# Start addresses of the up-projection's operand tiles in a hybrid decoder layer

## The chip, the core and the metric

The kernel runs on one core of a Trainium2 chip. The core has TensorE (matmul), VectorE, ScalarE and GpSimd, an on-chip memory SBUF of 128 partitions from which the engines read, a smaller memory PSUM into which TensorE writes, and DMA queues that move data between SBUF and the chip's main memory. The metric is the device time of one execution in microseconds (us); lower is better.

## What is computed

One decoder layer over 1024 positions of width 1024, in float32. Two groups of attention heads read the same normalised input; their outputs are joined, projected and added to the input; then comes an MLP with a squared ReLU:

```python
xn = rmsnorm(x, attn_norm_g)
proj = jnp.einsum('bsd,de->bse', xn, w_in)
...
x = x + jnp.einsum('bse,ed->bsd', mixed, w_out)
hn = rmsnorm(x, mlp_norm_g)
hid = jnp.square(jax.nn.relu(jnp.einsum('bsd,df->bsf', hn, w_up)))
x = x + jnp.einsum('bsf,fd->bsd', hid, w_down)
```

w_up is 1024 x 4096 and w_down 4096 x 1024.

## The kernel before

Every large product is made of matmuls in a rounded float32 type. To keep float32 accuracy each operand is split into a high and a low part (`split`, line 75: a copy into the rounded type gives the high part, a subtraction the low one), and a product is the sum of three matmuls: high by high, high by low, low by high. A matmul has a moving operand, which streams through the array, and a stationary one, the weights, which a separate load instruction puts into the array; here every matmul is preceded by its own load.

The stages are: an input projection; attention (lines 513 to 933), between whose pieces further projections and the first half of the output projection are woven; the rest of the output projection (from line 935); the **up phase** (`up`, line 1060, 16 calls); the **down phase** (`down`, line 1184, 16 calls).

Both MLP products use a Strassen-type scheme with seven products in place of eight. For the up phase the activations are prepared once: `bh[n]` and `bl[n]` (lines 967 to 969), n in the order UP = (1, 2, 3, 6, 7, 5, 4), are the high and low parts of seven combinations of quarters of the activations. These fourteen tiles, each of 4 x 512 floats per partition, are the moving operands. `up(j)` makes the seven combinations of weights of a block, splits each into a tile w with a high and a low half of 4 x 128 columns, and issues twelve matmuls per product (lines 1076 to 1079): for each of four k, w high by bh, w high by bl, w low by bh. That is 16 x 7 x 12 = 1344 matmuls of 512 columns.

All long-lived tiles come from `slot(tag, name, shape)`, line 146: tiles with the same tag share one place in SBUF, one after the other. Tags c0 to c13 lie in the pool "zr": bh and bl of the i-th product in UP are c(2i) and c(2i+1). Later the same tags hold the down phase's weight blocks (c0 to c9), two of its early operand sets and its running sums (c10 to c13). Tags w0 to w6 lie in the pool "zw", in the order of first use w2, w4, w3, two wor tiles, w0, w1, w5, w6. `w_slot` (line 1054) hands them out in rotation, seven tags for seven products, so that each product always gets the same tag: product 1 gets w5, 2 gets w6, 3 gets w0, 6 gets w1, 7 gets w2, 5 gets w3 and 4 gets w4. Before that, w0 and w1 hold the split weights of the output projection and w2 to w4 some of its other tiles; afterwards all seven hold blocks of the hidden values.

The order on each engine is the program's order, with priorities given by hand in the attention part; transfers are issued from SP's queue, for the down phase in a chain (`queue`, line 1157).

In the projection of line 458 the weights have 392 columns, the others 384; line 183 sets where the low half begins in its tile.

Of the kernel before, what the change touches and what calls it, by code (L numbers as in the profile page):

```python
# [16 lines left out]
P = 128  # L17
# [38 lines left out]
def hybrid_layer(  # L56
# [86 lines left out]
        tc.tile_pool(name="zl", bufs=1, side="left", reuse_waits="tile")  # L143
    )}

    def slot(tag, name, shape, dt=F32, pool=None):
        pool = o[pool or ("zw" if tag[0] == "w" else "zl")]
        return pool.tile([P] + shape, dt, tag=tag, name=name, bufs=1)


    X = [
        [slot(tag, "x", [2, 2, 512], F32R) for tag in tags]
        for tags in (("m1", "m2", "m3", "m4"), ("m0", "r0", "r1", "m5"))
    ]
# [705 lines left out]
    def mix_tiles(e):  # L860
        m = mixt[e] = slot(MIX[e], f"mix{e}", [2, S], F32R)
        mh[e], ml[e] = m[:, 0, :], m[:, 1, :]
# [7 lines left out]
    def out_weights(dt, e0):  # L870
        i = nout[0] = nout[0] + 1
        wr = o["zw"].tile([P, 4, P], F32, tag="wor", name="wor", bufs=2)
        nc.sync.dma_start(wr, w_o[dt][:, e0 : e0 + 4, :])
        w = slot(f"w{i % 2}", "wos", [2, 4, P], F32R)
        split(w[:, 0], w[:, 1], wr, nc.scalar, nc.gpsimd)
        return w[:, 0], w[:, 1]
# [154 lines left out]
    for dt in (1, 5, 2, 6, 3, 7):  # L1031
        w = out_weights(dt, 4)
# [273 lines left out]
    for i in range(len(STEPS)):  # L1306
        down(i)
        if STEPS[i][0] == len(PHASES) - 1 and late:
            name, dt, cs = late.pop(0)
# [65 lines left out]
```

## Time and profile before

| what | us |
|---|---|
| timed runs | 1091.99, 1091.10, 1089.88 |
| their median | 1091.1 |
| span of the profiled execution | 1090.4 |
| input projection and attention, to the last output product | 0 to 473 |
| up phase | 473.7 to 781 |
| down phase | 781 to 1086 |

The profiled execution is one more run; what is known of its time is the span, from its first to its last instruction. Rows of a view name the line, the engine and the tiles (written <- read, with buffer numbers left out). All matmuls of a helper have the helper's line, 73; what tells the phases apart is the tile they write: pu in the up phase, pd in the down phase, po in the output projection, ps and qps in the input projections. In a row of the timeline stand the start, the length and what ran; x8 says that eight instructions of one kind were merged. A matmul's own length covers its way through the array, and several are under way at once, so lengths of single matmuls overlap.

### The profile page before, as it was taken

The numbers are of one execution on the slowest core, as the hardware profiler recorded it, in microseconds if no ns is written. First come the engines' busy times: TensorE is split into PE (matmuls) and PEld (weight loads), VectorE is DVE, ScalarE is ACT, GpSimd is POOL, SyncE is SP. The second block draws the span as 40 slices with busy tenths as digits, with TensorE's granted clock in tenths as the row PEclk, the third lists the DMA queues.
The fourth block names the chain that finished last, engine by engine and source line by source line (L and its number), as shares of the span: only waits on it lengthen the run. The fifth ranks groups of instructions, "written<-read, shape, count | busy, mean of one in ns | idle before, by whom it ended". The sixth has DMA issues, their size and how long they took to land.

```text
span 1090.4 us, 15675 instructions
## 1 busy us (share of the span) xinstructions
PE 1080.1 (99%) x5556; PEld 933.8 (86%) x5556; DVE 782.7 (72%) x1321; ACT 571.4 (52%) x1022; POOL 362.4 (33%) x352
## 2 busy tenths in 40 slices
PE   9999999999999999999999999999999999999998
PEld 8999999999898888778888888888888888888886
DVE  8377677765776786898686869867665876674395
ACT  5558588776667766554545444353633433333331
POOL 4572523434445543333222232322212222231100
PEclk9999999999999999999999999999999999999999
DMA  9401212324657564663554543443998876665523
GB/s 292 156 22 53 69 36 65 113 70 150 230 164 252 182 209 173 212 231 126 193 184 174 188 160 135 149 170 145 335 390 308 305 288 224 237 231 177 176 87 116
DMA packets 96223, 195.69 MB, mean 179 GB/s; under 512 B 7392, under 2 KB 19856, under 8 KB 96144
## 3 DMA queue, kind: packets, MB, share of 16 engines
q1 hardware_dynamic: 95856, 194.54, 51.0%
q8 instruction: 44, 0.72, 0.3%
q14 instruction: 35, 0.29, 0.1%
q10 hardware_dynamic: 288, 0.15, 0.0%
HBM read 141.61 MB, written 53.04 MB: 179 GB/s over the span
## 4 chain that ended last, share of the span: by engine, by line
PE 86%; DMA 5%; DVE 4%; ACT 1%; issue 1%; POOL 1%; SPq 0%; DVEq 0%; ACTq 0%; POOLq 0%
PE pd L73 28%; PE pu L73 27%; PE ps L73 13%; PE po L73 4%; PE spb L73 3%; PE pvb L73 3%; PE tpb L739 3%; PE sp L73 1%; PE pv L73 1%; PE tpa L568 1%; DMA h_d<-h 1%; DMA xq<-in_x_dram 1%; DMA wr<-in_w_a_dram 1%; DMA rd_d<-rd 1%; PE ptk L334 1%
## 5 line engine op out<-in xcount | busy, mean ns | idle before, releaser
L73 PE MATMUL pd<-hx,wx 128*128 128x512 f32 (+1 forms) x1350 | 304.9, 388 | 0.0
L73 PEld LDWEIGHTS pd<-hx,wx 128*128 128x128 f32 x1350 | 252.7, 188 | 52.2
L73 PE MATMUL pu<-bh,wu 128*128 128x512 f32 x896 | 276.6, 390 | 0.3 <-POOL wu L80 0.2
L73 PEld LDWEIGHTS pu<-bh,wu 128*128 128x128 f32 x896 | 168.0, 188 | 36.1 <-POOL wu L80 0.6
L73 PE MATMUL ps<-w,x 128*128 128x384 f32 (+1 forms) x960 | 198.3, 344 | 0.5 <-ACT z L463 0.3
L73 PE MATMUL pu<-bl,wu 128*128 128x512 f32 x448 | 174.0, 389 | 0.0
L73 PEld LDWEIGHTS ps<-w,x 128*128 128x128 f32 x960 | 164.8, 189 | 3.8 <-ACT z L463 0.7
L77 ACT CAST hx<-hr 128x1024 fp32r<-128x1024 f32 x56 | 59.1, 1055 | 176.1 <-PE pd L73 170.9
L80 POOL TENSOR_TENSOR wx<-wda,wx 128x1024 fp32r<-128x1024 f32 x24 | 64.3, 2678 | 196.6 <-ACT wx L77 188.6
L80 DVE TENSOR_TENSOR hx<-hr,hx 128x1024 fp32r<-128x1024 f32 x56 | 72.5, 1302 | 72.5 <-ACT hx L77 72.5
L73 PEld LDWEIGHTS pu<-bl,wu 128*128 128x128 f32 x448 | 84.1, 188 | 17.7 <-issue 0.2
L73 PE MATMUL po<-mix,wos 128*128 128x512 f32 x384 | 94.2, 395 | 0.6 <-ACT pc L914 0.3
L73 PEld LDWEIGHTS po<-mix,wos 128*128 128x128 f32 x384 | 70.6, 188 | 15.7 <-ACT wos L77 1.1
L80 POOL TENSOR_TENSOR wu<-wus,wu 128x512 fp32r<-128x512 f32 x32 | 46.6, 1459 | 111.8 <-ACT wu L77 99.5
L80 POOL TENSOR_TENSOR wu<-wur,wu 128x512 fp32r<-128x512 f32 x32 | 44.1, 1378 | 102.7 <-ACT wu L77 100.1
L1047 DVE TENSOR_TENSOR ht<-hb 128x512 f32<-128x512 f32 x32 | 22.9, 757 | 62.8 <-ACT hb L1102 62.8
L80 POOL TENSOR_TENSOR w<-wr,w 128x384 fp32r<-128x384 f32 (+1 forms) x47 | 50.1, 1074 | 40.1 <-ACT w L77 28.6
L77 ACT CAST wu<-wus 128x512 fp32r<-128x512 f32 x64 | 37.9, 618 | 46.5 <-PE pu L73 39.2
L77 ACT CAST wx<-wda 128x1024 fp32r<-128x1024 f32 x56 | 58.5, 1049 | 6.8 <-DMA wda<-in_w_d_dram 6.5
L703 ACT ACTIVATE sb<-sb,nmb 128x128 f32<-128x128 f32 (+3 forms) x64 | 49.7, 778 | 22.1 <-DVE nmb L697 21.6
L406 DVE TENSOR_TENSOR ptl<-tpb,pth 128x512 fp32r<-128x512 f32 (+1 forms) x80 | 49.6, 631 | 15.1 <-ACT pth L405 14.3
L1101 ACT ACTIVATE hb<-hb 128x2048 f32<-128x2048 f32 x16 | 30.7, 1917 | 48.5 <-DVE hb L1050 48.4
(211 smaller groups left out, 1844.5 us busy)
## 6 DMA issues: line engine op xcount, KB each, us to landing
wda<-in_w_d_dram SPq DMA_DIRECT2D x34, 1024.0 KB, 8.7
hr<-hid_d SPq DMA_DIRECT2D x56, 512.0 KB, 5.7
wur<-in_w_u_dram SPq DMA_DIRECT2D x32, 512.0 KB, 4.4
hid_d<-ht SPq DMA_DIRECT2D x16, 1024.0 KB, 4.5
hid_d<-hb SPq DMA_DIRECT2D x16, 768.0 KB, 3.6
mix<-mixs_d SPq DMA_DIRECT2D x7, 1024.0 KB, 5.4
wr<-in_w_b_dram SPq DMA_DIRECT2D x32, 192.0 KB, 2.5
xq<-in_x_dram SPq DMA_DIRECT2D x8, 512.0 KB, 5.9
```

The source lines that it names most:

```text
L73: return nc.tensor.matmul(out, lhsT, rhs, start=start, stop=stop)
L77: hi_eng.copy(hi, src)
L80: lo_eng.tensor_tensor(out=lo, in0=src, in1=hi.bitcast(F32), op=ALU.subtract)
L334: nc.tensor.transpose(pt[:w, j * P : (j + 1) * P], x[:, 4 * c + j, col : col + w], ident)
L406: nc.vector.tensor_tensor(out=lo[:, cols], in0=pt[:, cols], in1=hi[:, cols].bitcast(F32), op=ALU.subtract)
L568: nc.tensor.transpose(tp[:, hh * P : (hh + 1) * P], pts[hh // 2][:, hh % 2, c0 : c0 + P], ident)
L703: nc.scalar.activation(pr[:, :nk], pr[:, :nk], AF.Exp, scale=-1.0, bias=nm[:, c : c + 1], accum_out=dn_b[p % 2][:, h, i : i + 1] if p < 3 ...
L739: nc.tensor.transpose(tp[:, c0 : c0 + P], probs[qi][:, kb * P : (kb + 1) * P], ident)
L1047: eng.tensor_tensor(out=out, in0=a, in1=b, op=ALU.subtract)
L1101: nc.scalar.activation(b, b, AF.Relu)
```

## The change

`slot` gets a table SHIFT. A tile whose tag is in it is allocated a little longer, and a view is handed out that begins SHIFT[tag] floats, 4 bytes each, behind the tile's start. The c tiles become 2112 floats long (8448 bytes in place of 8192), w2 becomes 1032 and w6 1056 floats long (in place of 1024). c9 and five of the w tags aren't in the table, and keep their length; what follows a longer tile in its pool moves along.

```diff
+    SHIFT = {
+        "w2": 8, "w6": 32,
+        "c0": 8, "c1": 40, "c2": 40, "c3": 8, "c4": 24, "c5": 56, "c6": 16,
+        "c7": 32, "c8": 48, "c10": 12, "c11": 20, "c12": 56, "c13": 24,
+    }
+
     def slot(tag, name, shape, dt=F32, pool=None):
         pool = o[pool or ("zw" if tag[0] == "w" else "zl")]
-        return pool.tile([P] + shape, dt, tag=tag, name=name, bufs=1)
+        if tag not in SHIFT:
+            return pool.tile([P] + shape, dt, tag=tag, name=name, bufs=1)
+        n, by = math.prod(shape), SHIFT[tag]
+        full = 1024 + by if tag[0] == "w" else 2048 + 64
+        t = pool.tile([P, full], dt, tag=tag, name=name, bufs=1)[:, by : by + n]
+        if len(shape) == 1:
+            return t
+        if len(shape) == 2:
+            return t.rearrange("p (a b) -> p a b", b=shape[1])
+        return t.rearrange("p (a b c) -> p a b c", b=shape[1], c=shape[2])
```

## The prediction

> **What bounds the kernel now.** I read the page's busy times first, then the chain of work that ended last in order of time, then the timeline of TensorE inside the up phase.
>
> ```profile
> PE 1080.1 (99%) x5556; PEld 933.8 (86%) x5556; DVE 782.7 (72%) x1321; ACT 571.4 (52%) x1022; POOL 362.4 (33%) x352
> PEclk9999999999999999999999999999999999999999
> L73 PE MATMUL pu<-bh,wu 128*128 128x512 f32 x896 | 276.6, 390 | 0.3 <-POOL wu L80 0.2
> L73 PE MATMUL pu<-bl,wu 128*128 128x512 f32 x448 | 174.0, 389 | 0.0
> ```
>
> TensorE is busy 99% of the span at full granted clock, and the 1344 up matmuls (896 with a high part bh moving, 448 with a low part bl) hardly wait for anybody. The 390 ns are one matmul's own duration; they overlap, so the price of one is the distance between two starts. The chain gives that:
>
> ```profile
> 487.15 178.00 PE pu L73 x784
> 665.15 1.72 PE pms L73 x4
> 666.86 114.29 PE pu L73 x504
> 781.15 300.57 PE pd L73 x1326
> 1081.75 0.71 DVE pd L1290
> ```
>
> From 487 to 1082 us the chain is nothing but matmuls: 178.00/784 = 227.0 ns each in the up phase, 300.57/1326 = 226.7 ns in the down phase. Whatever changes the distance between two starts in the up phase moves the end one for one; 1 ns on all 1344 is 1.34 us, or 0.12%. No other engine is near:
>
> ```profile
> 487.00:665.00 178.00, 177.85 (x785) 147.32 (x786) 135.96 (x193) 83.34 (x112) 53.67 (x40) 1.00 0.46 169
> ```
>
> This stretch has TensorE busy for 177.85 of 178 us, VectorE for 135.96, ScalarE for 83.34, GpSimd for 53.67.
>
> **What one matmul costs beside its columns.** Four runs of undisturbed matmuls, from the timeline of TensorE (start, length, matmuls in the row):
>
> ```profile
> 26.68 11.60 PE L73 MATMUL qps<-w,x 128*128 128x384 f32 x66
> 43.70 6.74 PE L73 MATMUL ps<-w,x 128*128 128x392 f32 x37
> 353.02 0.34 PE L73 MATMUL spb<-k2z,q1b 128*128 128x384 f32 x1
> 353.31 0.28 PE L73 MATMUL pvb<-ptl,vb 128*128 128x256 f32 x1
> ...
> 354.14 0.28 PE L73 MATMUL pvb<-pth,vb 128*128 128x256 f32 x1
> 500.20 0.62 PE L73 MATMUL pu<-bh,wu 128*128 128x512 f32 x2
> 500.65 0.39 PE L73 MATMUL pu<-bl,wu 128*128 128x512 f32 x1
> 500.88 0.62 PE L73 MATMUL pu<-bh,wu 128*128 128x512 f32 x2
> ```
>
> A row ends with the last matmul's own 0.34 us, so 384 columns cost (11.60-0.34)/65 = 173.2 ns and 392 columns (6.74-0.34)/36 = 177.8 ns. The 256-column row starts lie seven steps apart (six rows are left out): 0.83/7 = 118.6 ns. In the up phase the pattern high, low, high repeats after 0.68 us, so three cost 680 ns. From 512 against 384 a column costs (226.7-173.2)/128 = 0.418 ns; 512 columns are 213.9 ns, which leaves a **gap of about 12.8 ns per matmul** that isn't streaming. Each matmul loads new weights while its predecessor runs, so the gap may well come from two reads of SBUF at once. That gap is all that the change can touch: 1344 x 12.8 = 17.2 us.
>
> **The change, part by part.** (1) Addresses. No instruction, DMA or wait is written or dropped; slot() hands out a view that starts later in a longer tile, and SP's and POOL's queues keep their order. The allocator puts every w and c slot of the old kernel 224 bytes past a multiple of 256. The longer c slots are 8448 bytes, 33 x 256, so the tiles keep that base and the offsets alone count: bh1 0, bl1 128; bh2 128, bl2 0; bh3 64, bl3 192; bh6 32, bl6 96; bh7 160, bl7 224; bh5 16, bl5 48; bh4 192, bl4 64. w2 comes first in its pool, is 32 bytes longer and starts 32 later, so w0 to w5 all land on 0; w6 lands on 128. There are seven products and seven w slots in rotation, so product 2 always has w6 and the six others a slot at 0. Products 1 and 2 keep one moving tile at their weights' place and one 128 away; the five others (5 x 192 = 960 matmuls) get two new distances each.
>
> (2) What a distance is worth. The old up phase has one place for everything, so it can't show it. One place in the trace has another: line 183 puts the low weights w of the 392-column projection at column 400, 1600 bytes, thus 64 bytes off modulo 256, while 384-column ones lie at 1536, 6 x 256. There every third moving operand is at another place than its weights. By the terms above 392 columns should cost 392 x 0.418 + 12.8 = 176.7 ns; the row says 177.8, that is **1.1 ns more**, not less. (Since 392 columns also end differently, part of this may be length.) A gap that came from equal places should have shrunk there. The smallest gap in a row is that of the 256-column run, 118.6 - 107.0 = 11.6 ns, 1.2 less. The worst run of undisturbed up matmuls is this one, just after a wait:
>
> ```profile
> 477.20 0.40 PE L73 MATMUL pu<-bl,wu 128*128 128x512 f32 x1
> 477.44 0.63 PE L73 MATMUL pu<-bh,wu 128*128 128x512 f32 x2
> 477.91 0.39 PE L73 MATMUL pu<-bl,wu 128*128 128x512 f32 x1
> 478.13 0.63 PE L73 MATMUL pu<-bh,wu 128*128 128x512 f32 x2
> 478.60 0.39 PE L73 MATMUL pu<-bl,wu 128*128 128x512 f32 x1
> 478.83 0.40 PE L73 MATMUL pu<-bh,wu 128*128 128x512 f32 x1
> 479.06 0.39 PE L73 MATMUL pu<-bl,wu 128*128 128x512 f32 x1
> 479.29 0.62 PE L73 MATMUL pu<-bh,wu 128*128 128x512 f32 x2
> ```
>
> Nine steps in 2.09 us are 232.2 ns each, 5.5 above the steady 226.7, at unchanged places; afterwards the stream falls back into the 680 ns pattern. So the gap depends on how the two reads stand to each other in time, and a stream of equal matmuls settles on one rhythm. I expect the shifted streams to settle as well. Their price lies between 0 (same rhythm) and the 392 row's 1.1 ns on the 960 matmuls with new distances, 1.1 us; I take the middle, **+0.5 us**. Both ends of the whole range are -12.8 ns (gap gone) and +5.5 ns (never settled).
>
> The row first, then the rule: each matmul here carries its own weight load and 12.8 ns of gap. The Trainium skill, "TensorE: Matmul & The Clock Gate", Part 2, step 1, says that the array reads moving values and weights through two independent SBUF ports, so that loading weights takes nothing from a running matmul. By it the places are worth exactly 0 and the sum would be 1091.1. The gap in the trace is no proof against it, since it could be a fixed cost of exchanging weights.
>
> (3) The same slots outside the up phase. 15 of 16 wos weight tiles of the output projection are in w0 and w1 and move by 32 bytes against the mix tiles: 360 matmuls, at +1.1 ns 0.4 us, at +5.5 ns 2.0 us; I take 0, because their distance is constant and their stream is broken by attention pieces anyway. The second and fourth operand sets of the down phase lie in c10 to c13: 48 matmuls, 0.3 us at most. All other down operands stay.
>
> (4) The other engines read and write shifted tiles. Three wr buffers, 1568 bytes apart, already lie 32 bytes apart modulo 256, and the cast that reads them takes the same everywhere:
>
> ```profile
> L77 ACT CAST w<-wr x40: 494/511/532, 25.0 to 269.5; 128x384 fp32r<-128x384 f32 x32, 128x392 fp32r<-128x392 f32 x8
> ```
>
> 494 to 532 ns over 40 casts of two lengths leaves no room for a place effect above some 7%. I cost it at nothing: the cover is the 42 us by which VectorE is idle in the stretch above. 7% on its 136 us, 9.5 us, would still fit. The loads into c0 to c9 are issued a whole step ahead, and a step is 300.57/16 = 18.8 us against 8.7 us to land:
>
> ```profile
> wda<-in_w_d_dram SPq DMA_DIRECT2D x34, 1024.0 KB, 8.7
> ```
>
> **The sum.** 0 to 1.1 us on the path, taken as 0.5. The profiled span is 1090.4 us, so a span of 1090.9; the median of the timed runs is 0.7 above the span, so 1091.1 + 0.5 = **1091.6 us**.
>
> **The rivals.** *Rhythm lost (slower).* With bh and bl at different distances, the gap after each matmul differs, and the stream never settles. Place: the 960 matmuls of products 3, 6, 7, 5 and 4. Price: 5.5 ns each, +5.3 us, 1096.4; with products 1 and 2 too, 1344 x 5.5 = 7.4 us, 1098.5. It decides over 0.2% from 2.3 ns per affected matmul. For it: the run after 477.20, and 392 columns being dearer. Against: that the 392 stream, of mixed places, holds 177.8 over 37 matmuls. Chance 0.25.
>
> *Equal places were the collision (faster).* If the gap is two reads meeting in the same part of SBUF, and 224 against 224 is the worst case, the five products lose it: 960 x 12.8 = 12.3 us, 1078.8; half of it gives 1084.9. For it: the gap is there in all phases, and nearly all tiles share one place. Against: the 392 row, and that a stream sweeps all places modulo 256 within 64 of 512 columns, so a start 64 bytes later only moves the meeting. By the skill's same page, Part 2, "Back-to-back issue gap", 512 columns need N/2.4 + 2.5 = 215.8 ns, an estimate that would make it 1344 x 10.9 = 14.6 us, 1076.5; no row here shows such a distance with weights changing. Chance 0.18.
>
> *The change doesn't do what it says*: other places than I worked out, or work reordered because views replace tiles. With the path full of matmuls, 1091.1 again. Chance 0.05.
>
> **How the numbers follow.** Forecast 0.52, covering 1090 to 1093. With the third rival that is 0.57 within 0.2% of before, 2.2 us, which is about what a measurement of this kernel can tell from no change. Slower 0.25, faster 0.18. For eight in ten the range takes in the forecast, nearly all of the lost rhythm (to 1098) and the lesser gains (from 1087); it leaves out most of the removed collision and the dearest end of the lost rhythm.
>
> **What would show it.** In the chain of the changed kernel, the up rows divided by their count: 226.7 to 228 ns if I am right, 231 or more if the rhythm is lost, under 224 if a collision is gone. The timeline gives each product by itself, twelve matmuls in the order 1, 2, 3, 6, 7, 5, 4: products 1 and 2 should repeat every 680 ns. The down row must stay at 226.7. A different waiting list of TensorE, or VectorE near 100% of the up phase, would mean that I looked at the wrong engine.

## The result

The changed kernel takes 1096.94 us (median of 1096.94, 1097.46 and 1096.82) against 1091.1: 5.8 us more, a ratio of 1.0059 with a 95% interval of 1.004 to 1.0079. The forecast was 1091.6, the range 1087 to 1098. The time lies inside the range, where the slower rival stood (1096.4), and outside the 1090 to 1093 that the forecast itself covered.

The same groups of the page, after:

```profile
PE 1086.3 (99%) x5556; PEld 935.4 (85%) x5556; DVE 771.6 (70%) x1321; ACT 574.2 (52%) x1022; POOL 366.8 (33%) x352
PEclk9999999999999999999999999999999999999999
L73 PE MATMUL pu<-bh,wu 128*128 128x512 f32 x896 | 280.8, 394 | 0.0
L73 PE MATMUL pu<-bl,wu 128*128 128x512 f32 x448 | 176.1, 394 | 0.0
```

Counts and clock are as before, and TensorE waits even less; the matmuls themselves have become dearer. VectorE's busy time is 11 us lower, but that doesn't go with the step: in a run below whose up phase is as before (low tiles 256 bytes further) it is 772.5 us too. The chain of waits of the changed kernel (start, length, work, count):

```profile
472.83 194.47 PE pu L73 x840
...
669.02 116.68 PE pu L73 x504
785.70 300.81 PE pd L73 x1326
```

Length over count is 231.5 ns in both up rows, where the 504 matmuls after the break took 114.29/504 = 226.8 before. The down row is longer by 0.24 us. That accounts for the change: from the first to the last start of an up matmul the trace has 312.64 us after and 307.07 before, 5.57 more. At 4.7 ns more on 1344 matmuls it would be 6.3; the rest is that the slower stream no longer has to wait for its first weights (the row at 487.15 in the chain before began after such a wait; now one unbroken row starts at 472.83). The two spans, 1095.2 and 1090.4, differ by 4.8, since what precedes the up phase came out 1.0 us shorter in this profile; in the runs below the first up matmul starts at 471.6 to 474.4 us, without regard to the edit.

The timeline of the changed kernel, at a place where the old one repeated every 0.68 us:

```profile
500.25 0.62 PE L73 MATMUL pu<-bh,wu 128*128 128x512 f32 x2
500.71 0.40 PE L73 MATMUL pu<-bl,wu 128*128 128x512 f32 x1
500.95 0.63 PE L73 MATMUL pu<-bh,wu 128*128 128x512 f32 x2
501.41 0.40 PE L73 MATMUL pu<-bl,wu 128*128 128x512 f32 x1
501.65 0.62 PE L73 MATMUL pu<-bh,wu 128*128 128x512 f32 x2
502.11 0.39 PE L73 MATMUL pu<-bl,wu 128*128 128x512 f32 x1
502.33 0.63 PE L73 MATMUL pu<-bh,wu 128*128 128x512 f32 x2
```

From one bh row to the next it is 0.70, 0.70 and 0.68 us: no fixed period, and dearer nearly everywhere. What has to be explained is the place: is it where a tile lies, how consecutive moving tiles lie to each other, or how moving values lie to weights?

### The profile page after: what moved, and what is told of

Read it like the earlier page. It is cut to its first block, busy times and chain, and to the rows that moved or that the text cites. A ratio compares the mean times of both kernels' runs of the same rounds, so it can differ in the third digit from the quotient of the medians.

```text
span 1095.2 us, 15675 instructions
## 1 busy us (share of the span) xinstructions
PE 1086.3 (99%) x5556; PEld 935.4 (85%) x5556; DVE 771.6 (70%) x1321; ACT 574.2 (52%) x1022; POOL 366.8 (33%) x352
## 4 chain that ended last, share of the span: by engine, by line
PE 97%; DVE 1%; DMA 1%; ACT 1%; issue 0%; ACTq 0%; DVEq 0%
PE pu L73 28%; PE pd L73 27%; PE ps L73 15%; PE po L73 8%; PE spb L73 3%; PE pvb L73 3%; PE qps L73 3%; PE tpb L754 3%; PE sp L73 1%; PE pv L73 1%; PE tpa L583 1%; PE ptk L349 1%; PE ptq L349 1%; DMA mix_d<-mtb 0%; DMA xr<-in_xT_dram 0%
## 5 line engine op out<-in xcount | busy, mean ns | idle before, releaser
L73 PE MATMUL pu<-bh,wu 128*128 128x512 f32 x896 | 280.8, 394 | 0.0
L77 ACT CAST hx<-hr 128x1024 fp32r<-128x1024 f32 x56 | 58.9, 1051 | 176.8 <-PE pd L73 173.2
L420 ACT CAST pth<-tpb 128x512 fp32r<-128x512 f32 (+1 forms) x80 | 41.9, 542 | 23.2 <-PE tpb L754 17.9
```

Source lines behind the costliest of these rows:

```text
L73: return nc.tensor.matmul(out, lhsT, rhs, start=start, stop=stop)
L77: hi_eng.copy(hi, src)
L420: nc.scalar.copy(hi[:, cols], pt[:, cols])
```

## The experiments

All offsets are set in the table SHIFT. "Distance" is the start of the moving tile minus that of the weights, modulo 256 bytes. Steps per product are worked out from the trace: the starts of the 1344 up matmuls in order of time, twelve to a product, and a step is the time from one start to the next. Means leave out steps over 260 ns, which hold a wait; means of single products also leave out the first of the sixteen rounds, in which some matmuls run in another order. Times are set against runs of the kernel before on the same chip (medians 1090.8 to 1091.5).

**Each half of the change alone.** First the weights only:

```diff
     SHIFT = {
         "w2": 8, "w6": 32,
-        "c0": 8, "c1": 40, "c2": 40, "c3": 8, "c4": 24, "c5": 56, "c6": 16,
-        "c7": 32, "c8": 48, "c10": 12, "c11": 20, "c12": 56, "c13": 24,
     }
```

> Only the weights move (six w slots to 0, w6 to 128); all fourteen moving tiles stay at 224, so the moving place never changes from one matmul to the next. If the rhythm is lost because consecutive moving operands lie at different places: 226.7 ns per up matmul and 1091 us. If the distance between moving values and weights is what counts: 230 ns or more per up matmul and 1095 us or more.

Measured: 1099.8 us, ratio 1.0089 (1.0072 to 1.0106). Chain of waits and timeline of this run:

```profile
670.51 117.59 PE pu L73 x504
```

```profile
700.21 0.63 PE L73 MATMUL pu<-bh,wu 128*128 128x512 f32 x2
700.67 0.40 PE L73 MATMUL pu<-bl,wu 128*128 128x512 f32 x1
700.91 0.63 PE L73 MATMUL pu<-bh,wu 128*128 128x512 f32 x2
```

233.3 ns per matmul, and a period of 0.70 us for three. All moving tiles stay at one place, so no change from one moving operand to the next is needed: the distance to the weights alone costs 6.6 ns. And the stream isn't restless; it keeps a rhythm, a dearer one. Nor is it other engines' writing of the weights: the 848 steps of this run during which an engine writes a weight tile take 233.3 ns in the mean, the 492 others 233.4.

Then the moving tiles only (the line with w2 and w6 taken out):

> Only the moving tiles move, with the offsets of the change; the weights stay at 224. If consecutive moving operands at different places are the cause: the same as the changed kernel, some 231 ns per up matmul and 1096 to 1097 us. If the distance to the weights is the cause: also slower, but by other amounts per product, since all distances change by 32; products 1 and 2, now at distances 32 and 160, would differ from their 230 ns. If the moved weights alone are the cause: 226.7 ns and 1091 us.

1098.76 us, ratio 1.0079 (1.0064 to 1.0094). The products' means are 230.9 to 233.1 ns; products 1 and 2 went from 230.5 and 230.3 in the changed kernel to 232.7 and 232.1. By the steps (233.3 and 232.1 ns) each half is dearer than both together (231.5). That is what a price on distances gives, and not one on places.

**All at one place, but another.**

```diff
-        "w2": 8, "w6": 32,
+        "w2": 8,
-        "c0": 8, "c1": 40, "c2": 40, "c3": 8, "c4": 24, "c5": 56, "c6": 16,
-        "c7": 32, "c8": 48, "c10": 12, "c11": 20, "c12": 56, "c13": 24,
+        "c0": 8, "c1": 8, "c2": 8, "c3": 8, "c4": 8, "c5": 8, "c6": 8,
+        "c7": 8, "c8": 8, "c9": 8, "c10": 8, "c11": 8, "c12": 8, "c13": 8,
```

> All moving tiles and all weights of the up phase lie at 0 modulo 256. Both theories of distance (between consecutive moving operands, or between moving values and weights) expect the old rhythm: 226.7 ns per up matmul, 1091 us. If 224 was a good place by itself: 230 ns or more and over 1095 us. If 0 is a better place by itself: under 224 ns and under 1088 us.

1091.49 us, ratio 1.0005 (0.9995 to 1.0014). Chain and timeline:

```profile
665.39 114.30 PE pu L73 x504
```

```profile
699.73 0.61 PE L73 MATMUL pu<-bh,wu 128*128 128x512 f32 x2
700.18 0.39 PE L73 MATMUL pu<-bl,wu 128*128 128x512 f32 x1
700.41 0.61 PE L73 MATMUL pu<-bh,wu 128*128 128x512 f32 x2
```

226.8 ns and 0.68 us again. Neither the place 224, nor the longer tiles, nor the views cost or save anything.

**One distance, for the low tiles alone.** SHIFT holds the seven odd c tags, first with 32 floats (128 bytes), then with 64 (256 bytes).

> High moving tiles and weights at 224, every low moving tile 128 bytes further, in all seven products alike. If consecutive moving operands at different places lose the rhythm: 230 to 232 ns per up matmul, 1095.5 to 1098.5 us. If a rhythm of three matmuls can hold with one fixed distance: a steady period of 680 ns for three again and 1091 us; what the changed kernel lost would then come from changes between products.

> As the run with low moving tiles 128 bytes further, but 256 bytes further. If places count modulo 256: 226.7 ns per up matmul and 1091 us. If they count modulo 512 or more, or if the longer tiles are what costs: 230 ns or more and over 1095 us.

128 bytes: 1098.89 us, ratio 1.0076 (1.0061 to 1.0091), steps of 236, 234 and 230 ns over and over, 700 for three. 256 bytes: 1091.19 us, ratio 1.0006 (0.9997 to 1.0016), 680 for three. At 128 bytes neither outcome that was expected came: the period is steady, but a dearer one. One operand of three at a distance is as dear as all three in the run with moved weights, and places count modulo 256.

**Places change, distances don't.** SHIFT is `"w6": 32, "c2": 32, "c3": 32`.

> Product 2 alone has both its moving tiles and its weights at 96, all other products everything at 224: the distance from moving values to weights is 0 in each product, but the place changes twice in 84 matmuls. If the distance within a product is the cause: 226.7 ns inside product 2 and at most some 0.5 us more in all, 1091 to 1092 us. If any change of place loses the rhythm for long: 230 ns or more in products 2 and 3.

1091.63 us, ratio 0.9998 (0.9988 to 1.0007). Inside product 2 the steps are 226.7 ns. Two steps at either border are dear: the last matmul of product 1 takes 232.3 and the first of product 2 230.7. In the first of these the moving values and their own weights both lie at 224; only the weights then being loaded, product 2's, lie elsewhere. So the weights under load seem to be the ones that matter; but the moving place changes at the same border, and no run separates the two. The second of them has all its operands at 96 already and is dear all the same, so a step also depends on what went before it.

**Which distances?** Three runs give each product a distance of its own, for bh and bl alike, with the weights at 224.

> Weights at 224; high and low moving tiles of one product at the same place, but each product at its own distance from the weights: products 1, 2, 3, 6, 7, 5, 4 at 32, 64, 96, 128, 160, 192, 224 bytes. If any distance costs the same step as in the runs with one fixed distance: 233.3 ns per matmul in every product, about 1099 us. If the cost goes by the distance: different products settle at different steps of 6.7 ns, some perhaps at 226.7 or 220. If only the change of place between high and low counted: 226.7 ns and 1091 us, which the run with moved weights alone speaks against.

> The same with distances of 16, 48, 80, 144, 208, 240 and 8 bytes for products 1, 2, 3, 6, 7, 5, 4. If any distance costs a step: 233.3 ns in each, about 1099 us. If reads go in lines of 16, 32 or 64 bytes and only whole lines count: the 8-byte product stays at 226.7 while 16 or more costs a step, or 16 stays as well. A product under 226 ns would be a place worth taking.

> Distances just below 256: products 1, 2, 3, 6, 7, 5, 4 at 252, 248, 244, 236, 232, 228 and 20 bytes. If the moving read may lie up to 16 bytes behind the weights without loss: 226.7 ns in the first three products, more in the others. If 0 and 240 are two single good places: more than 226.7 ns in all. If the rhythm has a cheaper step: some product below 226 ns.

| run | distance: mean step in ns, by product in the order 1, 2, 3, 6, 7, 5, 4 | ratio |
|---|---|---|
| first | 32: 233.5, 64: 229.7, 96: 234.2, 128: 233.3, 160: 233.6, 192: 232.4, 224: 232.5 | 1.0081 (1.0064 to 1.0098) |
| second | 16: 232.2, 48: 233.0, 80: 231.3, 144: 233.3, 208: 234.2, 240: 226.7, 8: 232.6 | 1.0071 (1.0056 to 1.0086) |
| third | 252: 230.1, 248: 232.7, 244: 239.4, 236: 230.4, 232: 234.7, 228: 235.8, 20: 237.5 | 1.0099 (1.0083 to 1.0114) |

Since every product follows one at another distance, a number is the price in that company. No product went below 226.7 ns, and the one only 4 bytes before its weights (252) was 3 ns dearer. One distance looked free: 240, of product 5 in the second run, which goes at the old 226.7 ns in each of the last fifteen rounds. So 240 was given to all (60 floats for c0 to c13), and then to all but product 7, which kept the 208 it had in front of product 5:

> All moving tiles 240 bytes from their weights, in every product. If the 226.7 ns of the one product at 240 holds by itself: 226.7 ns throughout and 1091 us. If that product only kept a rhythm from its neighbours: 230 ns or more and over 1095 us.

> As the run with all moving tiles 240 bytes from their weights, but product 7 at 208. The product at 240 that follows one at 208 took 226.7 ns, the same distance throughout took 236.7. If a stream at one distance has more than one rhythm and keeps the one into which it is led: product 5, right after product 7, goes at 226.7 ns, and so perhaps do 4, 1, 2, 3 and 6, up to the next product 7. If the distance alone sets the time: 236.7 ns in all products at 240.

All at 240: 1104.12 us, ratio 1.0111 (1.0093 to 1.0128), the slowest of all. Chain:

```profile
674.50 119.27 PE pu L73 x504
```

That is 236.6 ns a matmul, or 0.71 us for three; the 226.7 of the one product doesn't hold by itself. With product 7 at 208: 1097.82 us, ratio 1.007 (1.0053 to 1.0087). The products at 240 have means of 230.2 to 230.4 ns, but none of them goes at 230: they take 226.7 ns in some rounds and 233.3 in others. Product 4 in the third round, then in the fourth:

```profile
531.43 0.39 PE L73 MATMUL pu<-bl,wu 128*128 128x512 f32 x1
531.65 0.61 PE L73 MATMUL pu<-bh,wu 128*128 128x512 f32 x2
532.11 0.39 PE L73 MATMUL pu<-bl,wu 128*128 128x512 f32 x1
```

```profile
550.67 0.40 PE L73 MATMUL pu<-bl,wu 128*128 128x512 f32 x1
550.91 0.63 PE L73 MATMUL pu<-bh,wu 128*128 128x512 f32 x2
551.37 0.40 PE L73 MATMUL pu<-bl,wu 128*128 128x512 f32 x1
```

Three matmuls take 0.68 us in the one and 0.70 in the other. From the second round on, the six products between one product 7 and the next (5, 4, 1, 2, 3, 6) keep one rhythm, and product 7 switches it: 226.7 ns before it gives 233.3 after it, and 233.3 gives 226.7. Only the break in the middle of the up phase interferes: behind it the products at 240 go at 236.7, and behind the next product 7 at 233.3. So one and the same distance goes at 226.7, 233.3 or 236.7 ns, by what ran before it. The expectation that a stream keeps the rhythm into which it is led is borne out; that product 7 leads it into 226.7 holds in 7 of these 15 rounds only, and 236.7 ns in all products at 240 is refuted.

**Was the row on which the forecast rested a matter of place?** The kernel before, with `lo = 400` for all weight tiles in line 183:

> The kernel before, with the low half of every projection weight tile at column 400, 64 bytes off modulo 256, also for 384 columns. If the place made the 392-column matmuls dearer: the 384-column ones leave 173.3 ns for 174 to 180 ns, and the kernel gets slower by 1 to 6 us. If their length did: 173.3 ns and 1091 us.

1090.75 us, ratio 1.0001 (0.9992 to 1.0011). The run of undisturbed 384-column matmuls in its timeline:

```profile
25.68 12.51 PE L73 MATMUL qps<-w,x 128*128 128x384 f32 x71
```

(12.51-0.34)/70 = 173.9 ns, against 173.2 before. The steps are no longer even, they go from 168 to 180 ns, but their mean rises by only 0.6. In the later projections of 384 columns (tile ps) the undisturbed steps have a mean of 174.6 ns in both kernels. This lies between the two outcomes that were expected: place spoils the rhythm here as well, but it hardly costs anything on this stream.

## Why the prediction was right, and where it was wrong

*The path.* Right: the distance between two starts goes into the end one for one. There are 5.6 us more in the up phase and 5.8 in the time. No other engine came near, down matmuls took 226.9 ns in the mean for 226.7 (0.24 us, all of it in the first 96, of which the second and the fourth 24 are the moved ones; 0.3 was allowed), and a few waits of TensorE went, worth 0.7 us.

*The addresses.* No trace shows an address, but the runs bear the working out: offsets from the same reckoning brought back 680 ns for three where they should meet modulo 256 (everything at 0, low tiles 256 bytes further, product 2 moved as a whole).

*The step that failed* is "What a distance is worth": "I expect the shifted streams to settle as well. Their price lies between 0 (same rhythm) and the 392 row's 1.1 ns on the 960 matmuls with new distances, 1.1 us; I take the middle". The price was 4.7 ns on all 1344, and the streams of the changed kernel didn't settle. So the time fell into the range by way of the rival; the forecast's own mechanism and its 0.5 us failed. The 392 row was no measure for the price: with the same 64 bytes on 384 columns the mean rises by 0.6 ns, while 512 columns with one operand of three at 128 bytes rise by 6.6. And a single stream with one odd place told nothing of the ones with every place. That row should have stayed a lower end; the trace held a better guide, the 232.2 ns of the run after a wait, which I used for the rival. Nor was its +5.5 ns an upper end for a stream that never settles: streams that do settle cost 6.6 ns (weights alone moved) and 9.9 (all at 240). (In the working, 0.418 ns times 512 is 214.0 and not 213.9, so the gap is 12.7; nothing hangs on it.)

*"Products 1 and 2 should repeat every 680 ns"* was wrong with it: they took 230.5 and 230.3 ns per matmul. A moving tile 128 bytes from its weights is no better than one at another distance.

*Rhythm lost.* The rival's sign and sum held (5.3 us for 5.6 in the up phase) by two errors that cancel: 5.5 ns on 960 matmuls was put down where it is 4.7 on 1344. That the sum came so near was luck. Its mechanism held in part. In the changed kernel no product has a steady period; but alternating places aren't the cause, since one fixed distance costs 6.6 ns with a perfectly steady period. Streams at one fixed distance do settle, mostly at 700 or 710 ns for three in place of 680.

*Equal places as the collision.* Refuted: of the 21 other distances that were tried none had a mean step below that of distance 0, and two places for it (224, 0) are alike. By the rule weighed in the prediction (the Trainium skill, "TensorE: Matmul & The Clock Gate", Part 2, step 1: two independent read ports, so that a weight load takes nothing from a running matmul) the run with moved weights alone should have been unchanged; its matmuls went from 226.7 to 233.3 ns, and here the measurement decides.

*The output projection* was costed at 0. Its matmuls went from 228.6 to 232.9 ns per step (steps under 260 ns) where the weights moved to 0 (in the changed kernel, with the weights alone moved, and with everything at 0): 360 x 4.3 = 1.5 us. In the last of these three, where the up phase is as before, the time is up by 0.05%, 0.5 us, with an interval that reaches from -0.5 to 1.5. So whether it costs something at the end isn't settled.

*What stays open.* Why 680 ns for three is reached at distance 0 in every run, why 240 has several rhythms, how a product at 208 switches between them, and why one operand of three at an offset costs 6.6 ns (128 bytes) at 512 columns and 0.6 ns (64 bytes) at 384. The runs show that it is the distance modulo 256 between moving values and weights, and the history of the stream; they don't show the mechanism. No version faster than the kernel before was found.

## What to carry to other kernels

Where each matmul loads new weights while the last one streams, as here, give moving tiles and weights the same start modulo 256 bytes, and check it after any edit that changes a tile's size, for a few bytes more in one tile move everything behind it in its pool. Read such a stream by starts, not by busy time: TensorE was 99% busy both at 227 and at 237 ns. And a single odd row is a poor price for a whole new pattern; when all streams of a trace share one setting, its effect is unknown, and the nearest disturbed run of the stream itself is the better guide, though no bound. Where a stream can have several rhythms, look at it round by round: a mean of 230 ns was made of 226.7 and 233.3.

## What was not expected of the hardware

A stream of 512-column matmuls in rounded float32, each with a new weight load, settled at 680, 700 or 710 ns for three, and at the same distance of 240 bytes 226.7, 233.3 and 236.7 ns per matmul were seen, by what preceded: twelve matmuls at 208 bytes switch the 72 that follow from 226.7 to 233.3 or back. Where both operands move together to another place, the dear steps are mostly those at the border (232.3 and 230.7 ns against 226.7). A shift of 256 bytes is none at all (680 ns); at 252, 4 bytes short of it, a product took 230.1.
